# The last token chunk before the mixer: order of its matmul units, of the next weight's cast and of row 2's root

## The chip, the cores and the metric

The kernel runs on one core of a Trainium2 chip. The metric is the device time of one execution in microseconds (us), as the median of several runs. The core's engines are TensorE (PE; its weight loads are PEld), VectorE (DVE), ScalarE (ACT), GpSimd (POOL) and SyncE (SP, which issues most of the DMAs). Each of them takes its instructions in the order in which they stand in its own list and waits where an operand is not ready.

## The reference

One decoder layer on 512 tokens of width 1024, in float32: a half-step SwiGLU block, a mixer of HGRN2 heads and mLSTM heads, and a second half-step SwiGLU block, each between two RMS norms.

```python
x = x + 0.5 * rms_norm(swiglu_ffn(rms_norm(x, norm_pre[0]), ffn1_w_in, ffn1_w_out), norm_post[0])
mixed = token_mixer(rms_norm(x, norm_pre[1]), w_mix_in, ...)          # HGRN2 and mLSTM heads
x = x + rms_norm(mixed, norm_post[1])
x = x + 0.5 * rms_norm(swiglu_ffn(rms_norm(x, norm_pre[2]), ffn2_w_in, ffn2_w_out), norm_post[2])
```

The place that matters here is the seam between the first line and the second: the output product of the first SwiGLU block, its post-norm and residual sum, the pre-norm of the mixer, and the first products with `w_mix_in`.

## The kernel before

**Precision.** Each fp32 operand is split in two parts of a rounded format. ScalarE casts the high part (for weights L289, for turned token rows L365), and VectorE subtracts it from the source to get the low part (L291, L366). A product is three passes: high by high, high by low, low by high. A weight of 128x1024 comes by one DMA of 512 KB from SP into one of three buffers `raw`, and its two parts go to one of four places in the buffer `w`. A place is free once the last matmul on the weight that lay there is done (`drop`), and a `raw` buffer once its low part is made.

**The output product of the first block** (`ffn_out`) makes its two column halves of 512 one after the other. In the second half the last four weights of the inner width are kept for the end and run chunk by chunk: chunk i is the 128 tokens of row i (0 to 3), so that the norms of one row can run beside the matmuls of the next. A *unit* is one weight `n` (0 to 3) on one column quarter `v` (0 or 1): six matmuls of 128x256 (`plain`, L1004) into the quarter's PSUM bank. A chunk has eight units.

**Behind each chunk** (`last`) come, for its row: `post1`, in which ScalarE squares the two banks with a sum along the row (L448), VectorE multiplies them by the gain (L496), GpSimd makes the statistic and its power -0.5 (L449, L453), and VectorE adds the result to the residual `xs` in two halves (L504); then `after`, which for rows 0 and 1 is the whole pre-norm and for rows 2 and 3 only its *root*: two squares of `xs` on ScalarE and the power on GpSimd. `trans` turns a normed row on TensorE (eight transposes, L359), and ScalarE and VectorE write its two parts to `xq`, where the mixer reads it. Row 0 is turned behind chunk 2, row 1 within chunk 3.

**The head of the mixer** (`head4`) starts directly behind chunk 3: passes of eight matmuls (L561) on the first four mixer weights, with rows 0 and 1 alone, and between them the transposes of rows 2 and 3, whose scaling (L476) was left to this point. The first pass needs the high part of the first weight and the high parts of rows 0 and 1, the second pass the low parts of the rows, the third the low part of the weight.

**The order.** The lists of the engines follow the order in which the code issues work; a scheduler moves instructions by priority, and `behind(...)` keeps what is issued in it behind named instructions. In chunk 3 the code takes the units as (v,n) = (0,0), (1,0), (0,1), (0,2), (0,3), (1,1), (1,2), (1,3). After the second unit the generator yields "free": the place in `w` of weight n=0 is then free, so the split of the first mixer weight is begun (`first_split`, the cast alone) and `after(2)`, the root of row 2, is issued behind that cast. Row 1 is turned when the v=0 quarter has one unit left.

Of the kernel before, what the change touches and what calls it, by code (L numbers as in the profile page):

```python
# [18 lines left out]
NT = T // P  # L19
# [99 lines left out]
class Layer:  # L119
# [146 lines left out]
    def split(self):  # L266

        nc = self.nc
        it = self.items.popleft()
        raw = self.raw[it.key]  # L270
        _, a, b = raw.shape
        if it.dst:
            w = it.dst()
        else:
            if self.wt is None:
                self.wt = self.wp.tile([P, 2 * D * WBUF + FRONT + PAD], F32R, name="w")
            if not self.slot and it.key[0] != "mix":
                self.free = deque(FREE2 if it.key[0] == "f2" else FREE)
            n, o = self.lie("out" if it.key[1] == "out" else "mix" if it.key[0] == "mix" and b == 512 else "any")
            self.free.remove(n)  # L280
            w = self.wt[:, o : o + 2 * D].rearrange("p (b k t) -> p b k t", b=2, k=a)
            self.slot[id(w)] = n, o, w
        hi, lo = self.both(w)
        if it.sums:
            raw, hi, lo = (self.flat(v)[:, QUARTER:] for v in (raw, hi, lo))
        self.ready.append((w, it.dst is not None))
        rows = it.rows
        if rows is None:
            self.cast = nc.scalar.copy(hi, raw)  # L289
            yield  # L290
            self.low = nc.vector.tensor_tensor(lo, raw, hi.bitcast(F32), op=ALU.subtract)  # L291
        else:
            for j in range(a):
                nc.scalar.activation(hi[:, j], raw[:, j], AF.Copy, scale=rows[:, j : j + 1])
            yield
            for j in range(a):
                nc.vector.scalar_tensor_tensor(
                    lo[:, j], raw[:, j], rows[:, j : j + 1], hi[:, j].bitcast(F32), op0=ALU.mult, op1=ALU.subtract
                )
        with self.behind(*self.hold):  # L300
            for out, other in it.adds:
                o, c = self.raw[out], self.raw[other]

                late = out[1] >= (HEAD if out[0] == "f1" else 1)
                added = (nc.vector if late else nc.gpsimd).tensor_tensor(o, o, c, op=ALU.add)  # L305
                if not late:
                    self.pooled = added
        self.load_due(self.done)
        self.done += 1
        yield  # L310
# [201 lines left out]
                stack.enter_context(self.tc.issue_after(i.ins))  # L512
            yield

    def last(self, mm, ys, pieces, g, after, trans, head, out=lambda i: (), cast=False):


        for i in range(NT):
            for left in mm(i):
                if left == "free":  # L520
                    self.first_split = self.split()
                    next(self.first_split)
                    with self.behind(self.cast):
                        after(i - 1)
                elif i == NT - 1 and left == 2:
                    trans(i - 2)
            self.post1(i, *ys[i], pieces(i), g, *out(i))
            if not (cast and i == 2):
                after(i)
            if i == 2:  # L530
                trans(0)
        head(trans)
# [32 lines left out]
    def head4(self, trans, scaled):  # L565

        self.head = []
        lows = [self.low]  # L570
        for _ in self.first_split:
            pass
        with self.behind(*lows, self.low):
            scaled(2, 0)
        with self.behind(self.added[0]):
            self.full_split()
            with self.behind(self.low):
                scaled(2, 1)
            self.full_split()
        scaled(3, 0)  # L580
        scaled(3, 1)
        with self.behind(self.normed[1]):
            self.feed()
        for t, m in ((0, 0), (0, 1), (0, 2), (1, 0), (1, 1), (2, 0), (1, 2), (2, 1), (2, 2), (3, 0), (3, 1), (3, 2)):
            self.head_pass(t, m)
            if (t, m) in ((2, 0), (2, 2)):
                trans(2 if m == 0 else 3)
# [48 lines left out]
    def after(self, p, t):  # L636


        had, bank, nc = self.had, self.bank, self.nc
        tt = lambda out, a, b, op: nc.vector.tensor_tensor(out, a, b, op=op)  # L640
        h0, h1 = self.half(t, 0), self.half(t, 1)
        if p in ("c2", "e2"):
            nc.scalar.activation(h0 if p == "c2" else h1, self.two_by(bank[p[0] + "1", t]), AF.Silu)
        elif p in ("c4", "e4"):
            h = h0 if p == "c4" else h1
            self.later.append(lambda: tt(h, self.two_by(bank[p[0] + "3", t]), h, ALU.mult))
        elif p == "p1":
            self.copied = nc.scalar.copy(h1, self.two_by(bank["p1", t]))
        elif p == "p2":
            nc.scalar.activation(h0, self.two_by(bank["p1", t]), AF.Silu)  # L650
        elif p == "p4":
            ps = bank["p5", t]
            tt(self.two_by(ps), self.two_by(ps), h1, ALU.subtract)
            def gate():
                nc.scalar.activation(ps, ps, AF.Silu)
                self.later.append(lambda: tt(h1, self.two_by(ps), h1, ALU.mult))
            if self.second and t in GATED:
                self.after_next = gate
            else:
                gate()  # L660
        elif p == "p5" and t < self.filled:
            u = self.u[t] = self.st("u")
            tt(self.two_by(u), self.two_by(bank["p5", t]), h1, ALU.subtract)
        elif p == "p5":
            q = bank["p6", t] = self.ps()
            tt(self.two_by(q), self.two_by(bank["p5", t]), h1, ALU.subtract)
        elif p == "p6" and t < self.filled:
            u = self.u[t]
            tt(u, bank["p6", t], u, ALU.add)
        elif p == "p6":  # L670
            c22 = bank["p7", t] = self.ps()
            self.c22 = [nc.scalar.copy(c22, bank["p6", t])]  # L672
            if self.after_next:
                with self.behind(*self.c22):
                    self.after_next()
                self.after_next = None
        elif p == "p7" and t < self.filled:
            tt(h1, self.two_by(bank["p7", t]), self.two_by(self.u[t]), ALU.add)
        elif p == "p7":
            nc.scalar.copy(h1, self.two_by(bank["p7", t]))  # L680
        elif p == "p3" and t < self.filled:
            c12 = bank["p6", t] = bank["p3", t]
            tt(c12, self.u[t], c12, ALU.add)
        if p in ("p3", "p2") and {("p3", t), ("p2", t)} <= had:
            self.later.append(lambda: tt(h0, self.two_by(bank["p6", t]), h0, ALU.mult))
# [278 lines left out]
    def ffn_out(self, gpost_row, scale, after, trans, head):  # L964
# [3 lines left out]
        nc, mm = self.nc, self.nc.tensor.matmul  # L968
        tt = lambda out, a, b, op: nc.vector.tensor_tensor(out, a, b, op=op)
        f = "f2" if self.second else "f1"  # L970
        OF, QF, LF = OUT[f], QUARTERED[f], LAST[f]
# [78 lines left out]
        def pieces(C, i):  # L1050
            c = slice(QUARTER * (i // 2), QUARTER * (i // 2 + 1))
            return [(C[i % 2][v][:, c], slice(QUARTER * v, QUARTER * (v + 1))) for v in range(2)]


        with self.behind(*([self.loaded] if self.second else [])):
            g = self.gain("gpost", gpost_row)
        if self.second:
            self.sums_due("f2", done=AHEAD)
        n = 0
        for half in range(2):  # L1060
            C = [[self.ps() for _ in range(2)] for _ in range(2)]
            M, T, left = None, None, len(QF[half])
# [28 lines left out]
            if half == 0:  # L1091
                ys = [self.post0(pieces(C, i), g, scale) for i in range(NT)]
# [12 lines left out]
        def chunk(i):  # L1105
            vn = [(v, n) for v in range(2) for n in range(LF)]
            if i == 0:

                vn.sort(key=lambda f: f[1])
            turns = [(v, LF - 1) for v in range(2)]  # L1110
            if i == NT - 1 and not self.second:

                vn.insert(1, vn.pop(LF))
                turns[0] = vn[LF - 1]
            for v, n in vn:
                plain(C, ws[n], hs[n], i, v, False)
                if v and i == NT - 1:
                    self.drop(ws[n])
                if v and n == LF - 1 and i == 0:
                    add(C, T, 0)  # L1120
                if i == NT - 1 and not self.second and (v, n) == (1, 0):
                    yield "free"
                if (v, n) in turns:
                    yield 2 - v

        self.last(chunk, ys, lambda i: pieces(C, i), g, after, trans, head, lambda i: (self.hf[:, 4 + i, :],), not self.second)
        self.holes()


# [844 lines left out]
```

## Time and profile before

| | |
|---|---|
| time, median of 3 runs | 931.04 us (930.81 to 931.5) |
| the profiled execution's own time | 929.95 us |
| its span | 928.2 us |
| TensorE busy | 919.2 us (99% of the span) |
| VectorE, ScalarE, GpSimd busy | 766.8, 524.2, 182.6 us |
| DMA moved | 145.42 MB |

The times in the trace are counted from the start of the span. Chunk 3 lies at 332 to 339 us, the mixer's head behind it to 352 us. A row of the timeline has its start, its length, the engine, the line and the operation, and in brackets how long the engine was idle before it and what ended that; a row that joins several instructions has their number behind x.

### The profile page before, as it was taken

To read this page: it belongs to the slowest core of one execution; us is meant where nothing else is said; L and a number is where in the kernel's file an instruction comes from. 1 tells how busy PE (TensorE), PEld (TensorE's weight loads), DVE (VectorE), ACT (ScalarE), POOL (GpSimd) and SP (SyncE) were. 2 spreads that over 40 slices of the span, in tenths; PEclk is the share of its full clock that TensorE was granted. 3 is DMA by queue.
4 is the path that set the end of the run, shared out by engine and by line. 5 is a ranking of instruction groups with operands and counts; after the bars stand their busy time and mean duration, and the time that the engine had idled before them with its cause. 6 is when DMAs were issued, how large, how long until landed. Compare 5 with 4: busy or idle time off the path is not lost.

```text
span 928.2 us, 18311 instructions
## 1 busy us (share of the span) xinstructions
PE 919.2 (99%) x7429; PEld 886.1 (95%) x7429; DVE 766.8 (83%) x994; ACT 524.2 (56%) x751; POOL 182.6 (20%) x252
## 2 busy tenths in 40 slices
PE   9999999999999999999999999999999999999997
PEld 7999999999999999998887887899999999999997
DVE  6899988889887876698757665799898989998886
ACT  7646455557566467956533445495455455756661
POOL 2531112111111045652321310304000000011002
PEclk9999999999999999999999999999999999999999
DMA  9255888766897834898842124352454435279542
GB/s 311 76 160 136 188 205 199 193 148 159 231 270 227 249 87 121 169 187 190 171 80 69 46 91 140 110 179 62 125 160 134 135 117 161 89 227 249 175 148 91
DMA packets 118768, 145.42 MB, mean 157 GB/s; under 512 B 7414, under 2 KB 91418, under 8 KB 118684
## 3 DMA queue, kind: packets, MB, share of 16 engines
q1 hardware_dynamic: 102716, 129.05, 45.3%
q0 software_dynamic: 15680, 14.69, 12.1%
q8 instruction: 58, 0.95, 0.4%
q10 hardware_dynamic: 288, 0.52, 0.2%
q14 instruction: 26, 0.21, 0.1%
HBM read 142.14 MB, written 31.46 MB: 187 GB/s over the span
## 4 chain that ended last, share of the span: by engine, by line
PE 98%; ACT 1%; DMA 0%; DVE 0%; issue 0%; DVEq 0%; POOLq 0%; POOL 0%; ACTq 0%
PE ps L621 46%; PE ps L1012 14%; PE ps L1004 9%; PE ps L550 6%; PE ps L193 5%; PE ps L195 5%; PE ps L194 5%; PE ps L1443 2%; PE ps L359 1%; PE ps L561 1%; PE ps L1536 0%; PE ps L1741 0%; PE ps L1714 0%; PE ps L1489 0%; DMA hf<-in_norm_pre_dram 0%; PE ps L1738 0%
## 5 line engine op out<-in xcount | busy, mean ns | idle before, releaser
L289 ACT CAST w<-raw 128x1024 fp32r<-128x1024 f32 x246 | 251.2, 1027 | 200.4 <-PE ps L621 90.7
L291 DVE TENSOR_TENSOR w<-raw,w 128x1024 fp32r<-128x1024 f32 x246 | 299.6, 1221 | 31.8 <-ACT w L289 29.9
L621 PE MATMUL ps<-xq,w 128*128 128x256 f32 x2016 | 237.2, 277 | 0.0
L621 PEld LDWEIGHTS ps<-xq,w 128*128 128x128 f32 x2016 | 232.9, 188 | 0.0
L621 PE MATMUL ps<-sq,w 128*128 128x256 f32 x1512 | 177.9, 276 | 0.3
L621 PEld LDWEIGHTS ps<-sq,w 128*128 128x128 f32 x1512 | 174.2, 188 | 0.9 <-ACT ps L672 0.9
L305 DVE TENSOR_TENSOR raw<-raw,raw 128x1024 f32<-128x1024 f32 x72 | 89.9, 1252 | 7.6 <-DMA raw<-in_ffn_w_in_dram 6.1
L1012 PE MATMUL ps<-w,hs 128*128 128x256 f32 x672 | 80.9, 276 | 0.0
L1004 PE MATMUL ps<-w,hs 128*128 128x256 f32 x672 | 79.0, 276 | 0.0
L1012 PEld LDWEIGHTS ps<-w,hs 128*128 128x128 f32 x672 | 78.3, 188 | 0.0
L193 PE MATMUL ps<-w,xq 128*128 128x512 f32 x192 | 77.9, 407 | 0.1
L1004 PEld LDWEIGHTS ps<-w,hs 128*128 128x128 f32 x672 | 77.4, 188 | 0.0
L194 PE MATMUL ps<-w,xq 128*128 128x512 f32 x192 | 74.9, 391 | 0.0
L195 PE MATMUL ps<-w,xq 128*128 128x512 f32 x192 | 74.8, 391 | 0.0
L550 PE MATMUL ps<-xq,w 128*128 128x256 f32 x480 | 57.6, 282 | 0.0
L550 PEld LDWEIGHTS ps<-xq,w 128*128 128x128 f32 x480 | 56.8, 189 | 0.5 <-issue 0.5
L944 POOL DMA_DIRECT2D f2sums<-in_ffn_w_out_dram x15 | 20.9, 1538 | 176.3 <-DMA f2sums<-in_ffn_w_out_dram 176.3
L884 ACT CAST hs<-hf 128x1024 fp32r<-128x1024 f32 x32 | 33.7, 1054 | 28.0 <-PE ps L1012 20.3
L885 DVE TENSOR_TENSOR hs<-hf,hs 128x1024 fp32r<-128x1024 f32 x32 | 39.1, 1223 | 9.0 <-ACT hs L884 8.4
L944 POOL DMA_DIRECT2D f1sums<-f1sums x26 | 22.5, 866 | 110.5 <-DMA f1sums<-in_ffn_w_out_dram 56.4
L193 PEld LDWEIGHTS ps<-w,xq 128*128 128x128 f32 x192 | 36.1, 188 | 8.5 <-issue 1.0
L195 PEld LDWEIGHTS ps<-w,xq 128*128 128x128 f32 x192 | 36.0, 188 | 8.1 <-DVE xq L366 0.3
(275 smaller groups left out, 1216.7 us busy)
## 6 DMA issues: line engine op xcount, KB each, us to landing
raw<-in_ffn_w_in_dram SPq DMA_DIRECT2D x98, 512.0 KB, 5.0
raw<-in_ffn_w_out_dram SPq DMA_DIRECT2D x44, 512.0 KB, 4.9
raw<-in_w_mix_in_dram SPq DMA_DIRECT2D x28, 512.0 KB, 7.5
raw<-f2sums SPq DMA_DIRECT2D x15, 512.0 KB
raw<-f1sums SPq DMA_DIRECT2D x13, 512.0 KB, 7.1
raw<-in_w_mix_out_dram SPq DMA_DIRECT2D x8, 512.0 KB, 3.7
f2sums<-in_ffn_w_out_dram SPq DMA_DIRECT2D x30, 128.0 KB, 5.6
f2sums<-in_ffn_w_out_dram SPq DMA_DIRECT2D x15, 256.0 KB, 5.4
```

The costliest lines, as they stand in the source:

```text
L193: mm(ps, sh, mh, start=start, stop=False, **kw)
L194: mm(ps, sh, ml, start=False, stop=False, **kw)
L195: mm(ps, sl, mh, start=False, stop=stop, **kw)
L289: self.cast = nc.scalar.copy(hi, raw)
L291: self.low = nc.vector.tensor_tensor(lo, raw, hi.bitcast(F32), op=ALU.subtract)
L305: added = (nc.vector if late else nc.gpsimd).tensor_tensor(o, o, c, op=ALU.add)
L550: mm(ps[:, u0:u1], w[:, a, k, :], self.xop(k, b, u0, u1), start=k + n + m == 0, stop=k == ND - 1 and n == 2, skip_group_check=True,)
L621: self.nc.tensor.matmul(ps[:, c], wb[b][:, k, v], left[d][:, k, :], start=first and a + n + k == 0, stop=n == 2 and k == KH - 1, skip_grou ...
L885: self.nc.vector.tensor_tensor(lo, src, hi.bitcast(F32), op=ALU.subtract)
L944: nc.gpsimd.dma_start(to[:, a:b], v, accum_op=ALU.add)
L1004: mm(out, a[kk][:, i * P : (i + 1) * P], w[:, b, kk, QUARTER * v : QUARTER * (v + 1)], start=begin and c == kk == n == 0, stop=kk == 1 and ...
L1012: mm(ps[:, QUARTER * c : QUARTER * (c + 1)], A[a][:, c], B[b], start=begin and c == n == 0, stop=n == 2, skip_group_check=True,)
```

## The change

The two yields for the last chunk and the hand-made order of its units go; what they did falls back to the general case. Chunk 3 takes its units as the other chunks do, all of v=0 and then all of v=1. Row 1 is turned when v=0 is complete. The root of row 2 is issued behind chunk 2, as for any other row. The first mixer weight is split, both parts, at the start of the head.

```diff
             for left in mm(i):
-                if left == "free":
-                    self.first_split = self.split()
-                    next(self.first_split)
-                    with self.behind(self.cast):
-                        after(i - 1)
-                elif i == NT - 1 and left == 2:
+                if i == NT - 1 and left == 2:
                     trans(i - 2)
             self.post1(i, *ys[i], pieces(i), g, *out(i))
-            if not (cast and i == 2):
-                after(i)
+            after(i)
...
         lows = [self.low]
-        for _ in self.first_split:
-            pass
+        self.full_split()
...
-            turns = [(v, LF - 1) for v in range(2)]
-            if i == NT - 1 and not self.second:
-
-                vn.insert(1, vn.pop(LF))
-                turns[0] = vn[LF - 1]
             for v, n in vn:
                 plain(C, ws[n], hs[n], i, v, False)
...
-                if i == NT - 1 and not self.second and (v, n) == (1, 0):
-                    yield "free"
-                if (v, n) in turns:
+                if n == LF - 1:
                     yield 2 - v
```

In the lists below the lines of the changed kernel are 7 lower from this place on (L997 for L1004). TensorE in chunk 3: `ps_233` is the bank of v=0, `ps_234` that of v=1, `hs_253` the activations of weight n=0, and the two transposes turn row 1. Before:

```order
L1004 MATMUL ps_233_3447<-w_274,hs_253_3771 128x256 x6
L1004 MATMUL ps_234_3448<-w_274,hs_253_3771 128x256 x6
L1004 MATMUL ps_233_3447<-w_274,hs_255_3778 128x256 x6
L1004 MATMUL ps_233_3447<-w_274,xq2_76 128x256 x2
L1004 MATMUL ps_233_3447<-w_274,xq3_77 128x256
L1004 MATMUL ps_233_3447<-w_274,xq2_76 128x256 x2
L1004 MATMUL ps_233_3447<-w_274,xq3_77 128x256
L359 MATMUL ps_305_4138<-ident_67,hf_2_113 128x128 x4
L359 MATMUL ps_306_4145<-ident_67,hf_2_113 128x128 x4
L1004 MATMUL ps_233_3447<-w_274,hs_256_3783 128x256 x6
L1004 MATMUL ps_234_3448<-w_274,hs_255_3778 128x256 x6
```

And with the change:

```order
L997 MATMUL ps_233_3447<-w_274,hs_253_3771 128x256 x6
L997 MATMUL ps_233_3447<-w_274,hs_255_3778 128x256 x6
L997 MATMUL ps_233_3447<-w_274,xq2_76 128x256 x2
L997 MATMUL ps_233_3447<-w_274,xq3_77 128x256
L997 MATMUL ps_233_3447<-w_274,xq2_76 128x256 x2
L997 MATMUL ps_233_3447<-w_274,xq3_77 128x256
L997 MATMUL ps_233_3447<-w_274,hs_256_3783 128x256 x6
L359 MATMUL ps_305_4137<-ident_67,hf_2_113 128x128 x4
L359 MATMUL ps_306_4144<-ident_67,hf_2_113 128x128 x4
L997 MATMUL ps_234_3448<-w_274,hs_253_3771 128x256 x6
L997 MATMUL ps_234_3448<-w_274,hs_255_3778 128x256 x6
```

The first v=1 unit has moved from second place to behind the transposes, and the last v=0 unit from behind them to ahead of them.

ScalarE beside chunk 3: `raw_252` is the first mixer weight, the squares of `xs` are the root of row 2, the casts to `xq0` and `xq1` are the turned row (row 0 in the first pair, row 1 in the second). Before:

```order
L365 CAST xq0_78<-ps_295_4086 128x4x128
L365 CAST xq1_75<-ps_296_4093 128x4x128
L289 CAST w_274<-raw_252_3740 128x1024
L448 ACTIVATE junk_299_4115,col_297_4113<-xs_74 128x512
L448 ACTIVATE junk_302_4120,col_300_4118<-xs_74 128x512
L365 CAST xq0_78<-ps_305_4138 128x4x128
L365 CAST xq1_75<-ps_306_4145 128x4x128
L448 ACTIVATE junk_309_4178,col_307_4176<-ps_233_3447 128x256
L448 ACTIVATE junk_312_4184,col_310_4182<-ps_234_3448 128x256
```

And with the change:

```order
L365 CAST xq0_78<-ps_303_4099 128x4x128
L365 CAST xq1_75<-ps_304_4106 128x4x128
L448 ACTIVATE junk_297_4088,col_295_4086<-xs_74 128x512
L448 ACTIVATE junk_300_4093,col_298_4091<-xs_74 128x512
L448 ACTIVATE junk_309_4177,col_307_4175<-ps_233_3447 128x256
L365 CAST xq0_78<-ps_305_4137 128x4x128
L365 CAST xq1_75<-ps_306_4144 128x4x128
L289 CAST w_274<-raw_252_3740 128x1024
L448 ACTIVATE junk_312_4183,col_310_4181<-ps_234_3448 128x256
```

The weight's cast has moved from ahead of row 2's root to behind row 1's casts, and the square of the v=0 bank to ahead of them. On VectorE the same two change places around row 1's low parts: the multiplication of the v=0 bank (L496) now stands ahead of them and the low part of `raw_252` (L291) behind. On ScalarE, too, the cast of the fourth mixer weight (`raw_321`) now stands behind both squares of row 3's root, not between them. GpSimd's and SP's lists keep their order.

More of the change, by code (lines that the diff above doesn't have):

```diff
@@ L288, in split @@
         if rows is None:
-            self.cast = nc.scalar.copy(hi, raw)
+            nc.scalar.copy(hi, raw)
             yield
@@ L513, in behind, with last @@
             yield
-    def last(self, mm, ys, pieces, g, after, trans, head, out=lambda i: (), cast=False):
+    def last(self, mm, ys, pieces, g, after, trans, head, out=lambda i: ()):
         for i in range(NT):
             for left in mm(i):
-                if left == "free":
-                    self.first_split = self.split()
-                    next(self.first_split)
-                    with self.behind(self.cast):
-                        after(i - 1)
-                elif i == NT - 1 and left == 2:
+                if i == NT - 1 and left == 2:
                     trans(i - 2)
             self.post1(i, *ys[i], pieces(i), g, *out(i))
-            if not (cast and i == 2):
-                after(i)
+            after(i)
             if i == 2:
@@ L1120, in chunk @@
                     add(C, T, 0)
-                if i == NT - 1 and not self.second and (v, n) == (1, 0):
-                    yield "free"
-                if (v, n) in turns:
+                if n == LF - 1:
                     yield 2 - v
-        self.last(chunk, ys, lambda i: pieces(C, i), g, after, trans, head, lambda i: (self.hf[:, 4 + i, :],), not self.second)
+        self.last(chunk, ys, lambda i: pieces(C, i), g, after, trans, head, lambda i: (self.hf[:, 4 + i, :],))
         self.holes()
```

## The prediction

> **What bounds the kernel now.** First the page's head and its chain of waits.
>
> ```profile
> span 928.2 us, 18311 instructions
> PE 98%; ACT 1%; DMA 0%; DVE 0%; issue 0%; DVEq 0%; POOLq 0%; POOL 0%; ACTq 0%
> ```
>
> The chain that ended last is TensorE for 98% of the span. A change outside TensorE's own list therefore costs time only where it makes TensorE wait, and can only gain what TensorE waits now. So the second view is the timeline of TensorE around the last chunk (the columns are start, length, engine and line).
>
> ```profile
> 332.11 2.37 PE L1004 MATMUL ps<-w,hs 128*128 128x256 f32 x18
> 334.31 0.87 PE L1004 MATMUL ps<-w,xq 128*128 128x256 f32 x6
> 335.02 1.04 PE L359 MATMUL ps<-ident,hf 128*128 128x128 f32 x8
> 335.81 1.62 PE L1004 MATMUL ps<-w,hs 128*128 128x256 f32 x12
> 337.27 0.84 PE L1004 MATMUL ps<-w,xq 128*128 128x256 f32 x6
> 337.95 0.84 PE L1004 MATMUL ps<-w,hs 128*128 128x256 f32 x6
> 338.63 5.87 PE L561 MATMUL ps<-xq,w 128*128 128x256 f32 x48
> 344.35 1.03 PE L359 MATMUL ps<-ident,xn 128*128 128x128 f32 x8
> ...
> 348.84 2.98 PE L561 MATMUL ps<-xq,w 128*128 128x256 f32 x24
> ```
>
> No row has an idle mark: chunk 3 (332.11 to 338.6), the head of the mixer (from 338.63) and the transposes between them run without a gap. There is nothing here to gain. The question is only whether the former order feeds the head in time. What the head's first matmul needs is made on ScalarE:
>
> ```profile
> 333.80 1.05 ACT L289 CAST w<-raw 128x1024 fp32r<-128x1024 f32 x1 [0.77 <-PE ps L1004]
> 334.84 0.63 ACT L448 ACTIVATE junk<-xs 128x512 f32<-128x512 f32 x1
> 335.65 0.63 ACT L448 ACTIVATE junk<-xs 128x512 f32<-128x512 f32 x1
> 336.18 0.19 ACT L448 ACTIVATION_READ_ACCUMULATOR junk<-xs 128x1 f32 x1
> 336.27 1.05 ACT L365 CAST xq<-ps 128x512 fp32r<-128x512 f32 x2
> 337.22 0.39 ACT L448 ACTIVATE junk<-ps 128x256 f32<-128x256 f32 x1
> ```
>
> The row at 333.80 is the cast of the first mixer weight (raw_252). It ends at 334.85, 3.7 us ahead of the head, in a hole of 0.77 us before the squares of row 2's root.
>
> **The change, part by part.** The work is the same: 48 matmuls of chunk 3, the same casts, squares and DMAs. Only places move.
>
> **TensorE's list.** The first v=1 unit goes from second place to behind the transposes of row 1. The sum of chunk 3 is unchanged (48 matmuls, 8 transposes), so its end stays at 338.6. Cost 0 by itself: the v=0 bank is merely complete earlier, at 335.0 and not at 336.5.
>
> **ScalarE's list.** The weight cast must wait for the first v=1 unit, which frees its place in the weight buffer. That unit now begins at 335.81 and lasts half of the 1.46 us to the row at 337.27, so it ends at 336.54; in the present order the unit ended about 333.57 (two of three equal parts of 332.11 to 334.31) and the cast began 0.23 later. So the cast could begin at 336.77. But it also moves behind the squares of the root, the square of the v=0 bank and the two casts of row 1 turned. I lay these end to end with the steps that these rows give:
>
> ```profile
> 330.70 0.19 ACT L448 ACTIVATION_READ_ACCUMULATOR junk<-xs 128x1 f32 x1
> 330.92 0.39 ACT L448 ACTIVATE junk<-ps 128x256 f32<-128x256 f32 x1
> 331.20 0.20 ACT L448 ACTIVATION_READ_ACCUMULATOR junk<-ps 128x1 f32 x1
> 331.88 0.19 ACT L448 ACTIVATION_READ_ACCUMULATOR junk<-ps 128x1 f32 x1
> 331.97 1.06 ACT L365 CAST xq<-ps 128x512 fp32r<-128x512 f32 x2
> ```
>
> The root's squares wait for VectorE's residual sums and stay at 334.84 and 335.65, with the last read at 336.18. Read to next square takes 0.22 (330.70 to 330.92): 336.40. Square to its read 0.28: 336.68. Read to cast 0.09 (331.88 to 331.97): 336.77. Two casts until the next starts 0.95 (336.27 to 337.22): 337.72, later than the 336.77 of the buffer, so the queue decides. The weight cast lasts 1.05: it ends at **338.77**.
>
> **The start of the head.** TensorE's first weight load there, and what such a wait costs where the trace already has one:
>
> ```profile
> 338.52 5.77 PEld L561 LDWEIGHTS ps<-xq,w 128*128 128x128 f32 x48
> 677.34 0.64 PEld L621 LDWEIGHTS ps<-xq,w 128*128 128x128 f32 x5
> 677.65 0.57 ACT L672 COPY ps<-ps 128x512 f32<-128x512 f32 x1 [2.08 <-PE ps L621]
> 678.27 0.88 PEld L621 LDWEIGHTS ps<-sq,w 128*128 128x128 f32 x7 [0.29 <-ACT ps L672]
> ```
>
> At 677.65 ScalarE ends at 678.22 and TensorE goes on at 678.27, 0.05 later. So the head's load, due at 338.52, comes at 338.77 + 0.05 = 338.82: **0.30 us of waiting**, in a place where TensorE does not wait now. The five loads at 677.34 would have been followed after five steps of 0.12 (5.77 over 48), at 677.94; the next came at 678.27, so a wait shown as 0.29 cost 0.33. Bounds: 0.15 if the square starts 0.09 behind the read as the casts do, 0.13 sooner than above; 0.80 if the chain slips by another small square with its read, 0.28 + 0.22. A gain is excluded by the rows above without idle time. I take 0.30, the end that the steps in this same stretch give.
>
> **VectorE's list.** The multiplication of the v=0 bank goes ahead of row 1's low parts, and the weight's low part behind them.
>
> ```profile
> 335.33 1.28 DVE L366 TENSOR_TENSOR xq<-ps,xq 128x512 fp32r<-128x512 f32 x2
> 336.52 1.22 DVE L291 TENSOR_TENSOR w<-raw,w 128x1024 fp32r<-128x1024 f32 x1
> 338.86 0.41 DVE L496 TENSOR_TENSOR hf<-ps,gpost 128x256 f32<-128x256 f32 x1
> 339.19 0.74 DVE L476 SCALAR_TENSOR_TENSOR xn<-xs,col,gpre 128x512 f32<-128x512 f32 x1
> 343.20 0.75 DVE L476 SCALAR_TENSOR_TENSOR xn<-xs,col,gpre 128x512 f32<-128x512 f32 x1
> ```
>
> The multiplication waits for its square's read: 336.93 to 337.34. The low parts (1.28) follow to 338.65. The head wants them for its second pass, 8 steps of 0.12 behind 338.82: 339.78. The weight's low part starts with the cast's end: 338.82 to 340.04, wanted for the third pass at 340.74. Both are hidden, by 1.1 and 0.7 us. If those covers were gone each would be paid in full. Behind it in VectorE's queue: the scaling of row 2's first half 339.96 to 340.70, the v=1 multiplication to 341.04, then the residual sums of row 3, which wait for GpSimd's power.
>
> ```profile
> 331.06 0.27 POOL L449 TENSOR_SCALAR col<-col,col 128x1 f32<-128x1 f32 x1 [0.69 <-ACT junk L448]
> 332.97 0.86 POOL L453 TENSOR_TENSOR col<-col,nhalf 128x1 f32<-128x1 f32 x1
> 336.54 1.33 POOL L449 TENSOR_SCALAR col<-col,col 128x1 f32<-128x1 f32 x1 [0.69 <-ACT junk L448]
> 340.15 0.55 POOL L453 TENSOR_TENSOR col<-col,nhalf 128x1 f32<-128x1 f32 x1
> ```
>
> GpSimd's 0.27 us step took 1.33 at 336.54, exactly while VectorE made a weight's low part (336.52 to 337.74). With the low part moved to 338.82, it falls on the v=1 statistic (0.50 long at 339.56 now, ended 340.06), which then ends about 340.15; the power lies beside a scaling (L476) as at 332.97 and takes 0.86: 341.1, against 340.70 now. Row 3's residual sums come 0.4 us late, and so does the scaling of row 2's second half behind them (343.20 to 343.95 now, about 344.4 then). The head's transposes of it begin with a load at 344.24 + 0.30 (0.11 ahead of the row at 344.35, as at 338.52 and 338.63) and want that half 0.44 later, at 344.98: 0.6 us of cover. In return the root of row 2, freed from the low part, is ready at 337.5 and not 338.5, which nobody waits for. The Trainium skill's page "GPSIMD Engine Reference", section Specifications, says that GpSimd shares its SBUF interfaces with VectorE and contends with instructions that have two SBUF inputs; the rows at 336.54 and 332.97 agree, since both VectorE instructions read two tiles of SBUF. By that rule taken to its end the power would be held for the whole 0.74 of the scaling, not for 0.31 of it, and the cover would shrink from 0.6 to 0.2; the sum would stay 0.30.
>
> **SP's queue.** No entry changes place, but the load into raw_252's buffer (the fourth mixer weight, raw_321) waits for that weight's low part.
>
> ```profile
> 337.77 0.38 SPq L250 DMA_DIRECT2D raw<-in_w_mix_in_dram  x1
> 340.29 0.35 SPq L160 DMA_DIRECT2D gpost<-in_norm_post_dram  x1
> 342.20 1.03 ACT L289 CAST w<-raw 128x1024 fp32r<-128x1024 f32 x1
> DMA to landing us min/median/max: 7.5/9.1/10.6
> ```
>
> It is issued at 340.08, 2.3 us later. Now its cast runs at 342.20, so it lands within 4.4 us; in the changed kernel by 344.5. ScalarE's queue has the cast behind both squares of row 3's root (done about 343.5), with row 2's casts behind it, to 345.6. TensorE wants it at 348.84 + 0.30 less the 0.11 by which a load leads: 349.0. Hidden by 3.4 us. The two loads behind it on SP wait for low parts that move by 0.3 to 0.4 and are wanted long after. Everything later shifts with TensorE.
>
> **Sum.** 928.2 + 0.30 = 928.5 of span, 929.95 + 0.30 = 930.25 in the profiled execution. That one lies 1.09 below the median of the runs (931.04), so on the median the forecast is 931.04 + 0.30 = **931.3**. This is 0.03%; about 0.2% (1.86 us) is what a measurement of this kernel can tell from no change, so this counts as the same.
>
> **Rivals.**
> *No wait at all* (931.0): if the square of the v=0 bank slips in between the root's two squares, or the lags are 0.3 shorter, the cast meets 338.52. For it: the cover is short by only 0.3. Against: ScalarE keeps its order, and the root's second square waits for VectorE. Chance 0.15.
>
> *The late reload* (slower): the 512 KB load that is issued 2.3 us later takes as long as other loads of its form, 7.5 to 10.6 us in the answer on this tile between 325 and 440. Place: the head's fourth weight, wanted at 349.0; less 1.05 of cast and 0.05, it decides from a landing at 347.9, 7.8 us after issue. At 9.1 us the cast ends at 350.23 and TensorE waits 1.3, in all 931.04 + 0.30 + 1.3 = 932.6; at 10.6 it waits 2.8, in all 934.1. More than 0.2% it becomes from 9.4 us. For it: the gain for the post-norm (512 KB, too) would follow within 1 us, at the end of the v=1 multiplication (341.04), where it now has 2.5. Against: the load itself took at most 4.4 us. Chance 0.2, counted whole as slower.
>
> *GpSimd held longer* (931.9): the power is held for one more low part (1.22), the transposes wait 1.22 less 0.6: 0.6 more. Chance 0.08.
>
> *Faster*: nothing in the rows offers 1.86 us, as TensorE has no gap here. Left at 0.05 for what the trace doesn't show. A slip of the head's later weights that no row places gets 0.07, slower.
>
> **The numbers.** Forecast 0.45, no wait 0.15, GpSimd 0.08: together 0.68 for the same. Late reload 0.2 and the unplaced slip 0.07: 0.27 slower. Faster 0.05. The range begins below the no-wait case by the spread of the runs (930.81 is 0.23 under the median, and the forecast's runs spread alike): 930.6. At the top it takes in the reload up to 10.4 us, 933.9. The forecast's own range is 931.0 to 931.8.
>
> **What would show it.** In the changed profile: the weight cast after the two casts of row 1, at about 337.7; an idle mark of 0.3 us on the head's first weight load, released by that cast; the raw_321 load issued near 340.1 and its cast before 346; no other idle mark on TensorE until 352; the rest shifted by one constant. Wrong would be: no mark at the head, a mark of over 0.8 us, a second one at the transposes of row 2 or at the fourth weight, or a time outside the range.

## The result: faster by 2.1 us, outside the forecast

| | before | after |
|---|---|---|
| time, median of 11 runs each | 930.87 us (930.05 to 932.75) | 928.76 us (928.53 to 930.75) |
| ratio, with its 95% interval | | 0.9979 (0.9971 to 0.9987) |
| span of the profiled execution | 928.2 us | 927.7 us |

The kernel with the former order is faster by 0.21%; the forecast was no measurable change, with 930.6 as the lower end of its range. The seam itself behaves almost as forecast. TensorE there in the timeline of after (start, length, engine, line; everything lies 0.54 later than before, since chunk 3 starts at 332.65 and not at 332.11 in this execution):

```profile
338.39 0.76 PEld L997 LDWEIGHTS ps<-w,hs 128*128 128x128 f32 x6
338.50 0.84 PE L997 MATMUL ps<-w,hs 128*128 128x256 f32 x6
339.44 5.54 PEld L555 LDWEIGHTS ps<-xq,w 128*128 128x128 f32 x48 [0.30 <-ACT w L289]
339.44 5.74 PE L555 MATMUL ps<-xq,w 128*128 128x256 f32 x48
```

In before the same six loads are

```profile
337.84 0.76 PEld L1004 LDWEIGHTS ps<-w,hs 128*128 128x128 f32 x6
```

The head's first load carries the idle mark of 0.30, released by the weight's cast. From the first of the last six loads of chunk 3 to the head's first load it is 1.05 (338.39 to 339.44), where before had 0.68 (337.84 to 338.52): the new wait costs 0.37. (The rows of the matmuls would give 0.26, but behind the wait the first matmul is shown at the start of its load.) The rest of the seam, on the other engines, in the same timeline:

```profile
337.00 0.39 ACT L448 ACTIVATE junk<-ps 128x256 f32<-128x256 f32 x1
337.38 1.07 ACT L365 CAST xq<-ps 128x512 fp32r<-128x512 f32 x2
338.32 1.07 ACT L289 CAST w<-raw 128x1024 fp32r<-128x1024 f32 x1
339.42 1.23 DVE L291 TENSOR_TENSOR w<-raw,w 128x1024 fp32r<-128x1024 f32 x1
340.87 0.87 POOL L453 TENSOR_TENSOR col<-col,nhalf 128x1 f32<-128x1 f32 x1
340.68 0.38 SPq L250 DMA_DIRECT2D raw<-in_w_mix_in_dram  x1
344.73 1.05 ACT L289 CAST w<-raw 128x1024 fp32r<-128x1024 f32 x1 [0.59 <-DMA raw<-in_w_mix_in_dram]
```

The gain lies behind it. The chain of waits of before, then of after (start, length, what), with the mixer's matmuls (L550, in after L544) and two places much later:

```profile
345.38 2.83 PE ps L561 x24
351.83 33.97 PE ps L550 x288
387.58 2.12 PE ps L550 x18
390.56 14.84 PE ps L550 x126
408.45 5.47 PE ps L550 x48
602.84 5.61 PE ps L621 x48
809.45 5.44 PE ps L1004 x48
```

```profile
346.05 2.83 PE ps L555 x24
352.50 32.64 PE ps L544 x288
386.92 2.12 PE ps L544 x18
389.90 14.30 PE ps L544 x126
407.25 5.47 PE ps L544 x48
601.52 5.61 PE ps L614 x48
808.87 5.44 PE ps L997 x48
```

The same 288 matmuls take 1.33 us less (118.0 to 113.3 ns each), the same 126 take 0.54 less (117.8 to 113.5). The next 48 are equal. From the last six matmuls of chunk 3 to the mixer's first piece of the chain it is 13.88 before (337.95 to 351.83) and 14.00 after (338.50 to 352.50), 0.12 more: the wait's 0.37, less 0.25 by which the head's own matmuls are quicker. So the change is worth 0.37 - 0.25 - 1.33 - 0.54 = -1.75 us between chunk 3 and 408, inside the interval of the ratio (-1.2 to -2.7). The two spans differ by only 0.5 because of the 0.54 ahead of chunk 3 and of 0.74 lost in after between 602 and 809, where before is 1.32 behind at the first mark and 0.58 behind at the second. Neither lies in what the change moves; the kernel with the split at the head, below, takes 206.72 us over the second stretch, before 206.61 and after 207.35.

TensorE is never idle in this stretch in either kernel, and the clock is the same. The windows by engine (window, us, PE, PEld, DVE, ACT, POOL busy with the count of instructions, PE clock, DMA), of before and of after:

```profile
352.00:400.00 48.00, 48.00 (x405) 47.52 (x404) 33.89 (x50) 41.14 (x46) 28.38 (x46) 1.00 0.70 139
```

```profile
352.00:400.00 48.00, 48.00 (x420) 47.52 (x419) 33.30 (x49) 42.16 (x47) 28.50 (x46) 1.00 0.70 141
```

At a granted clock of 1.00 and full busy time in both, TensorE starts 405 instructions before and 420 after. It is a matter of pace, not of waiting.

**Where the slow pace begins.** Taken load by load, the starts of the weight loads in the trace of before are 113 ns apart at the end of chunk 3. From the head's first load they are 120 apart for 24 loads, those on raw_252, and 118 for the next 24, on two other weights. Between the head's two sets of transposes 24 loads run at 118, and behind the second set the pace is back at 113. It becomes 120 again with the mixer's first 24 matmuls, again on raw_252, and stays at 118 to the end of the 126, on weights that have nothing to do with it. In after the head's 48 (behind their first loads), the 288 and the 126 run at 113. Two stretches run at 118 in after as well, with no bad place near: the 24 between the transposes (2.83 us in both kernels) and the 18 between the 288 and the 126 (2.12 in both). The lists name the buffer `w` and not the place in it. The code's `lie` chooses that place when a weight is split, from those that are free then:

```python
LIES = {"any": (0, -16, -80, 48), "mix": (-16, 0, -80, 48), "out": (-80, 48, 0, -16)}
```

Before splits raw_252 while the other places are still taken, and all that fits is element 16 (96 - 80). After splits it at the head, and it gets element 96 (96 + 0). Of the weights cast into this buffer raw_252 is the only one whose place the change moves: in the two built programs 24 matmuls of the head and 24 of the mixer read their weight at another address, and no others do.

### The profile page after: what moved, and what is told of

It is laid out like the page before. It is cut to its first block, busy times and chain, and to the rows that moved or that the text cites. A ratio compares the mean times of both kernels' runs of the same rounds, so it can differ in the third digit from the quotient of the medians.

```text
span 927.7 us, 18311 instructions
## 1 busy us (share of the span) xinstructions
PE 918.1 (99%) x7429; PEld 885.0 (95%) x7429; DVE 766.5 (83%) x994; ACT 524.5 (57%) x751; POOL 183.4 (20%) x252
## 4 chain that ended last, share of the span: by engine, by line
PE 59%; DVE 2%; DMA 1%; issue 1%; ACT 1%; DVEq 0%; POOLq 0%; POOL 0%; ACTq 0%
PE ps L614 19%; PE ps L1005 8%; PE ps L544 6%; PE ps L193 5%; PE ps L195 5%; PE ps L194 5%; PE ps L997 4%; PE ps L1429 2%; PE ps L555 1%; DMA raw<-in_ffn_w_in_dram 1%; PE ps L359 1%; DVE w L291 1%; PE ps L1522 0%; PE ps L1727 0%; PE ps L1700 0%
## 5 line engine op out<-in xcount | busy, mean ns | idle before, releaser
L291 DVE TENSOR_TENSOR w<-raw,w 128x1024 fp32r<-128x1024 f32 x246 | 299.5, 1221 | 30.0 <-ACT w L289 28.7
L997 PE MATMUL ps<-w,hs 128*128 128x256 f32 x672 | 79.2, 276 | 0.0
L997 PEld LDWEIGHTS ps<-w,hs 128*128 128x128 f32 x672 | 77.5, 188 | 0.0
L544 PE MATMUL ps<-xq,w 128*128 128x256 f32 x480 | 55.7, 277 | 0.0
L544 PEld LDWEIGHTS ps<-xq,w 128*128 128x128 f32 x480 | 54.9, 188 | 0.5 <-issue 0.5
```

The costliest lines, as they stand in the source:

```text
L544: mm(ps[:, u0:u1], w[:, a, k, :], self.xop(k, b, u0, u1), start=k + n + m == 0, stop=k == ND - 1 and n == 2, skip_group_check=True,)
L997: mm(out, a[kk][:, i * P : (i + 1) * P], w[:, b, kk, QUARTER * v : QUARTER * (v + 1)], start=begin and c == kk == n == 0, stop=kk == 1 and ...
```

## The experiments

Each was timed against runs of before on the same chip (930.55, 930.62 and 930.77 us in the three sessions). "Place" is the first element of raw_252 in `w`.

**After, with raw_252 at before's place.**

```diff
+        self.mixed = False
...
             n, o = self.lie(...)
+            if it.key[0] == "mix" and not self.mixed:
+                self.mixed, o = True, 16
```

> The changed kernel, with one thing put back: the first mixer weight (raw_252) lies at element 16 of the weight buffer, as before, and not at 96. Every list of instructions is that of the changed kernel. Place theory (the weight at 16 makes TensorE's matmuls on it start every 120 ns instead of 113, and the slower rhythm then holds on for the weights behind it): the gain goes, time 930.8 to 931.2, about before or 0.3 over it since the wait at the head stays; the mixer's 480 matmuls of 128x256 take 57.6 us busy again. Wait theory (the 0.3 us wait at the head sets the rhythm anew, the place doesn't matter): 928.8, 55.7 us. Order theory (the order of the units does it): 928.8.

931.2 us, ratio 1.0007 (0.9998 to 1.0016). Its chain:

```profile
338.14 0.96 ACT w L292
339.14 5.96 PE ps L558 x48
352.42 33.97 PE ps L547 x288
391.15 14.84 PE ps L547 x126
```

The order of after is kept, its wait for the cast too (the chain passes over ScalarE at 338.14), and the gain is gone: 33.97 and 14.84 as before. The order alone does not make the kernel faster.

**Before, with raw_252 at element 0**, the same edit with 0 for 16.

> The kernel before, with the first mixer weight at element 0 of the weight buffer and not at 16 (64 bytes lower; 96 is not free at that time for its low part). Lists as before. Place theory: faster than before by 2.0 to 2.4 us (928.5) if only the very same place relative to the activations hurts, no change if 64 bytes aside hurt as well. Wait theory and order theory: no change, 930.9.

928.86 us, ratio 0.9979 (0.9970 to 0.9988): all of the gain, with the lists of before.

```profile
339.50 5.44 PE ps L564 x48
352.26 32.64 PE ps L553 x288
389.66 14.30 PE ps L553 x126
```

These two runs settle the cause of the difference: the place of one weight. Why a place sets the pace they do not show.

**Before, with the split at the head, and nothing else of the change.**

```diff
                 if left == "free":
-                    self.first_split = self.split()
-                    next(self.first_split)
-                    with self.behind(self.cast):
-                        after(i - 1)
+                    after(i - 1)
...
-        for _ in self.first_split:
-            pass
+        self.full_split()
```

> The kernel before with its order of units and its place of row 2's root, but the first mixer weight is split at the start of the head, as in the changed kernel; with that it lies at 96, and its cast stands behind row 2's root and ahead of row 1's casts, so that the head should not wait or wait under 0.1 us. Place theory: 928.4 to 928.8, faster than before by 2.0 to 2.4 and not slower than the changed kernel; rhythm 113 ns in the mixer. Wait theory: 930.9, as there is no wait at the head. Order theory: 930.9, as the units stand as before.

928.61 us, ratio 0.9974 (0.9964 to 0.9984).

```profile
339.31 5.44 PE ps L558 x48
352.07 32.64 PE ps L547 x288
```

Here raw_252 gets element 96 by itself, as in after, and its cast (336.80 to 337.83) stands ahead of row 1's casts, so the head does not wait. Its median is 0.15 under that of after, less than the intervals can tell.

**Before, with the general order of units alone**: the four lines that set `vn` and `turns` for the last chunk are taken out, raw_252 stays at 16.

> The kernel before with only the units of chunk 3 in the general order (all of v=0, then all of v=1); the first weight is still split when its place is free and lies at 16. Place theory: about before, 930.7 to 931.3 (the cast is later, so up to 0.3 of waiting). Order theory: 928.8. Wait theory: 928.8 if the head waits, else 930.9.

931.6 us, ratio 1.0011 (1.0002 to 1.0020): about 1 us slower. Part of it shows in the timeline at the transposes of row 2:

```profile
338.49 0.63 ACT L448 ACTIVATE junk<-xs 128x512 f32<-128x512 f32 x1
340.10 0.39 ACT L448 ACTIVATE junk<-ps 128x256 f32<-128x256 f32 x1
342.09 0.55 POOL L453 TENSOR_TENSOR col<-col,nhalf 128x1 f32<-128x1 f32 x1
344.01 1.22 DVE L291 TENSOR_TENSOR w<-raw,w 128x1024 fp32r<-128x1024 f32 x1
345.14 0.75 DVE L476 SCALAR_TENSOR_TENSOR xn<-xs,col,gpre 128x512 f32<-128x512 f32 x1
346.00 0.42 PEld L359 LDWEIGHTS ps<-ident,xn 128*128 128x128 f32 x4 [0.56 <-PE ps L359]
```

Row 2's root still stands behind the cast of raw_252 on ScalarE, and the cast now starts at 337.54. So the squares of the root start at 338.49, those of row 3's banks only at 340.10, and GpSimd's power for row 3 ends at 342.64, where before had 340.70. On VectorE the residual sums of row 3 wait for it, behind them come the low part of the second mixer weight (344.01) and the scaling of row 2's second half (345.14, 343.20 before), and the last four transposes of row 2 start late. Of these 1.94 us, 0.75 are the lag of this execution (the head's first load is at 339.27, 338.52 before); the rest uses up the cover at the transposes. From the head's start to the mixer it takes 13.73 (339.38 to 353.11) instead of 13.20 (338.63 to 351.83). A cast that comes late on ScalarE can thus cost time by way of GpSimd and VectorE, though TensorE has the weight in time. The 288 take 33.97 us here too: with raw_252 at 16 the order of the units brings none of the gain.

**Before, with raw_252 taken last of the four in the mixer.** The pace is slow on 390 matmuls that do not touch raw_252. Do they only inherit it?

```diff
-            for a in range(2):
-                w, ps = self.head[2 * p + a]
-                self.in_mm(ps, w, 256, 512)
...
+        for t in (1, 2, 3, 0):
+            w, ps = self.head[t]
+            self.in_mm(ps, w, 256, 512)
...
```

> Before's lists and before's place (16) of raw_252, but the forget gates take their four weights in the order 2, 3, 4, raw_252, so that 72 of the mixer's first matmuls run ahead of the 24 on raw_252. Theory 'carried': the 24 matmuls on raw_252 set a slow rhythm, which later matmuls keep on weights that lie well. Then the 72 that now come first run at 113.3 ns instead of 118, 72 x 4.6 = 0.33 us less; the 24 on raw_252 and what follows stay at 120 and 118 ns, the group of 126 at 14.84 us; the mixer group goes from 57.6 to 57.3 us, the time from 930.55 to about 930.2. Rival 'own': each of these matmuls is slow for a reason of its own (their operands, or where they stand in the program), which raw_252's place switches for all of them: the 72 stay at 118 ns, the group at 57.6 us, the time at 930.5. A third outcome, that the slow rhythm is gone also after raw_252, would say that the 24 cannot start it from where they now stand: 55.9 us and 928.9.

```profile
352.76 33.65 PE ps L550 x288
391.18 14.84 PE ps L550 x126
```

The 288 take 0.32 us less, as the carried pace would have it. Load by load: 113 ns for the first 72, 120 for the 24 on raw_252, then 118 to the end of the 126. The 72 are the matmuls that were at 118 when raw_252 went ahead of them. So the 192 behind raw_252 in this group inherit the pace. For the 126 the word says less: the 18 ahead of them run at 118 in after too, and there the 126 run at 113. In the runs with `xq` in its place they are slow wherever raw_252 lies at 16 and nowhere else, but how it reaches them is open. The time, 930.56 us at a ratio of 0.9999 (0.9990 to 1.0009), is too coarse for 0.3 us.

**Before, with all four of the head's weights 80 elements ahead of their usual place.**

> Before with all four of the head's weights placed 80 elements ahead of their slots' usual place (16, 2064, 4112, 6160) instead of raw_252 alone. Theory 'carried': a slow rhythm is there already, so the other three weights only go from 117.8 to 120 ns: 72 matmuls in the mixer (0.16 us) and up to 72 in the head (0.2 to 0.5 us, since 18 of them ran at 113 before): 930.9 to 931.2. Rival 'a share for each weight': one badly placed weight cost about 2.1 us against the well placed kernels, so four cost four times as much, some 937 us.

```profile
339.06 5.76 PE ps L564 x48
352.31 34.13 PE ps L553 x288
391.21 14.84 PE ps L553 x126
```

930.65 us, ratio 1.0002 (0.9993 to 1.0011). The 48 run at 120.0 ns and the 288 take 0.16 us more. Four badly placed weights cost no more than one, as far as the times can tell, because the pace was slow already.

**Before, with raw_252 at 8 and at 12.** One execution each: 928.37 and 928.07 us.

> Before with raw_252 at element 8 of the weight buffer, 32 bytes ahead of its place at 16; element 0 ran at 113 ns. If only the exact place of 16 (the same remainder as the moving operand's tiles) is bad, the mixer group is at 55.7 us and the time near 928.8; if a stretch around it is bad, 57.6 us and 930.5.

> Before with raw_252 at element 12, 16 bytes ahead of its place; 8 was fast and 16 slow. If only the exact coincidence counts, the mixer group is at 55.8 us and the time near 928.5; if the slow stretch begins between 8 and 12, 57.6 us and 930.5.

The chain of the first, then of the second:

```profile
339.00 5.52 PE ps L564 x48
351.84 32.72 PE ps L553 x288
```

```profile
338.80 5.54 PE ps L564 x48
351.66 32.74 PE ps L553 x288
```

Between 0 (32.64) and 16 (33.97) both lie close to 0. The loads on raw_252 itself are 116.7 ns apart at 8 and 117.4 at 12, so it has a price of its own there too, but the pace is back at 113 directly behind them. The own price thus comes at places where nothing is inherited, and what is inherited is most of the loss at 16.

**Before, with the moving rows `xq` 160 bytes further on**, the weight buffer where it was.

```diff
+        self.prm = self.cp.tile([P, 36], F32, name="prm")
         xq = {n: self.cp.tile(...) for n in (1, 2, 3, 0)}
...
-        self.prm = self.cp.tile([P, 36], F32, name="prm")
```

> Before with its lists and with raw_252 at element 16, but a small tile of parameters now lies ahead of the turned rows xq instead of behind them, so that xq lies 160 bytes further on; the weight buffer stays where it was. Theory 'pair': what is slow is the place of the weight against that of the moving rows (a kept weight at element 16 has the same remainder of its address by 512 as xq had). Then the matmuls on raw_252 run at 113 ns, the mixer group falls from 57.6 to about 55.8 us and the time to about 928.8, unless another weight now meets xq's new remainder and slows another stage. Rival 'weight alone': place 16 is slow by itself, whatever it is multiplied with: 57.6 us and 930.5.

952.29 us, ratio 1.0234 (1.0217 to 1.0251). The costliest group of the page and the mixer's, in before and then here (last column: busy time, mean ns of one, idle time before):

```profile
L621 PE MATMUL ps<-xq,w 128*128 128x256 f32 x2016 | 237.2, 277 | 0.0
L550 PE MATMUL ps<-xq,w 128*128 128x256 f32 x480 | 57.6, 282 | 0.0
```

```profile
L621 PE MATMUL ps<-xq,w 128*128 128x256 f32 x2016 | 248.6, 282 | 0.0
L550 PE MATMUL ps<-xq,w 128*128 128x256 f32 x480 | 58.7, 283 | 0.0
```

The expected 55.8 for the mixer did not come; its reservation did, in most stages. Load by load, raw_252's 24 matmuls in the mixer went from 120 to 117.3 ns, though the pace ahead of them was slow (119.7 for the last 24 loads of the head); the 264 behind them, on weights that ran at 113 in after at the same elements, run at 120.0. So the bad place has passed from raw_252 to its neighbours, although no weight moved. What counts is therefore not a place in the weight buffer by itself but the weight's place against that of the rows. Whether raw_252 would run at 113 behind a quick stretch can't be read here.

## Why the prediction was wrong

**The wait at the head: right.** Forecast 0.30; the mark shows 0.30, the step from load to load grew by 0.37. The order on ScalarE (square, two casts, weight cast), its steps and the lag came out within 0.1 us, once the 0.54 of this execution is taken off.

**The low parts, GpSimd and the reload: right.** VectorE's low part of raw_252 was laid at 338.82 (with the 0.54, 339.36) and starts at 339.42. The power was to end at 341.1 (341.64) and ends at 341.74. The raw_321 load was to be issued at 340.08 (340.62) and is at 340.68; it lands within 4.05, as its cast waits for it to 344.73, and TensorE never misses it. None of these adds a wait on TensorE until the mixer. So the rivals "no wait", "late reload" and "GpSimd held longer" did not happen in after. The wait at row 2's transposes that the last of them describes does appear with the general units alone (0.56), there because row 3's squares come late on ScalarE.

**The step that failed: "Everything later shifts with TensorE", the term put at nothing.** "Cost 0 by itself", said of chunk 3, holds: from its first matmul to its last six it takes 5.84 before (332.11 to 337.95) and 5.85 after (332.65 to 338.50). What failed is the same thought for the matmuls behind it. The prediction said that "only places move" and meant places in a list; from that it took that a change outside TensorE's list "can only gain what TensorE waits now", that "nothing in the rows offers 1.86 us, as TensorE has no gap here", and that the rest would be "shifted by one constant". All of these rest on a matmul of one shape costing the same wherever its weight lies. It does not: 113.3 ns or 118.0 over 288 of them, with the same shape, clock and engine time. With this term the prediction's sum would have been 931.04 + 0.37 - 0.25 - 1.33 - 0.54 = 929.3. The forecast made for an unmoved weight holds: after with raw_252 at 16 came to 931.2, where 931.3 was forecast.

**What could have been seen.** The quoted evidence had the clue. The prediction worked with steps of "0.12 (5.77 over 48)" and did not ask why 48 matmuls of the same shape took less elsewhere. The chain of before shows both:

```profile
223.36 5.44 PE ps L1004 x48
338.80 5.71 PE ps L561 x48
```

5.44 is 113 ns each, 5.71 is 119. A group whose instructions cost 5% more than another of the same shape, at a clock of 1.00, may hide a gain, though no idle mark stands at it. And in the code the change moves the moment of the split, on which `lie` decides. The order tells which buffer an instruction reads, not where in it.

## What to carry to other kernels

"Busy" is not "at full pace": compare the time per instruction of groups with the same shape before saying that an engine without gaps has nothing to gain. Where a buffer's places are given out as they come free, a change of order is also a change of addresses; list which operands move, and hold the place fixed in one run to part the two. A bad place should be judged by what runs behind it as well as by its own matmuls.

## What the runs showed of the hardware

Two things were not expected. The first is that a 128x256 matmul with its own weight load starts every 113 to 120 ns, by where the weight lies in SBUF against the moving rows: at elements 0 and 96 of the buffer 113, at 8 116.7, at 12 117.4, at 16 120. In the kernel's layout the weight at 16 and `xq` have the same remainder of their addresses by 512 bytes (160). That is not the whole of it: with `xq` 160 bytes further on, the weights at 96 and its like have a remainder 160 off that of `xq` and run at 120.0 as well. Which function of the two addresses counts, the runs do not show. The Trainium skill's page "TensorE: Matmul & The Clock Gate", section "Step-by-step: what each phase is for", says that TensorE has two independent SBUF read ports, and that loading the next weight does not take read bandwidth from the running matmul. These runs show a dependence between the two operands all the same: the 48 of the head 5.44 us with raw_252 at 0, 5.71 at 16. Whether it comes from the reading of SBUF they do not show.

The second is that a slow pace can outlast its cause. Behind 24 matmuls at 120 ns, 390 others on well placed weights ran at 118, with other products between them, and put in another order the 72 that now came ahead of the cause ran at 113. A bad place is not the only thing that starts such a stretch. Behind the head's first set of eight transposes 24 loads run at 118 in after too, and in the kernels with raw_252 at 0, 8 and 12; behind the second set the pace is 113 in all of these and in before. What starts, carries and ends the slow pace was not found, and no run tried to break it.
